# HGRN2 scores: one 128x128 product of rearranged key and query blocks per chunk in place of three small products

## The chip, the cores and the metric

The kernel runs on one core of one Trainium2 chip. The metric is the device time of one execution in microseconds (us). A core has a matrix engine, TensorE (PE in the profile; PEld is its weight load), and four others: VectorE (DVE), ScalarE (ACT), GpSimd (POOL) and SyncE (SP, which starts most transfers). Each works off its own list of instructions in order; they meet at semaphores. A matrix product takes its stationary operand as weights, streams the columns of the moving operand past it, and writes to PSUM, a small memory of eight banks; DVE and ACT copy results from there to SBUF, the working memory.

## What is computed

The reference is one inference step of a two-layer encoder trunk over 1024 prompt frames and 32 sample frames, model width 1024. Layer 0 mixes with HGRN2, a gated linear recurrence with 8 heads of 128x128 state; layer 1 with a short convolution; each is followed by an MLP. The part that the change touches is the recurrence:

```python
b = jnp.cumsum(gj, axis=-2)
qt = qj * jnp.exp(b)
kt = kj * jnp.exp(-b)
A = jnp.where(mask, jnp.einsum('bhtk,bhsk->bhts', qt, kt), 0.0)
o = jnp.einsum('bhtk,bhkv->bhtv', qt, S) + jnp.einsum('bhts,bhsv->bhtv', A, vj)
S = jnp.exp(bL[..., 0, :])[..., None] * S + jnp.einsum('bhsk,bhsv->bhkv', kj * jnp.exp(bL - b), vj)
```

The reference steps through blocks of 16 frames. The kernel takes chunks of 128 frames; the sums are the same, with other groupings of the decay factors.

## The kernel before, in words

All activations lie transposed, features on the 128 partitions, frames along the row. Layer 0 works on pairs of heads (`pr` = 0 to 3). Each pair runs four projections on TensorE (forget gate, value, query, output gate). The forget gate, query and output gate go head by head over three groups of 384, 384 and 288 columns, 24 products in a group: 8 input blocks by three passes over weights and inputs that are split in a high and a low part. Between those groups TensorE does the recurrence of the pair's two heads in six numbered steps (`step`, line 458): step 0 is `scores` of the first four chunks, step 1 `scores` of the other four and `states` of the first, step 2 the sample's scores, `outs` and `states`, step 3 `outs` and the sample's `outs`, steps 4 and 5 turn the outputs back (`o_turn`). The list `todo` (line 570) says after which group of columns a step is put: in pairs 0 to 2 step 0 of the first head follows the second column group of the second head's query projection. I name the places by letters. A is (h0,0), B is (h0,1), C is (h0,2), D is (h0,3), E is (h0,4) with (h1,0), F is (h0,5) with (h1,1), G is (h1,2). So `scores` is called at A, B, E and F: 4 calls in a pair, 16 in all, 4 chunks in a call, 64 chunks.

Within a chunk of 128 frames the scores are a 128x128 matrix (keys down, queries across), of which the lower triangle in time is wanted. One product of K and F (line 385) gives the whole matrix, and is right in the four 32x32 blocks on the diagonal. The blocks off the diagonal need other decay factors, so `carry` (lines 332 to 339) makes rescaled copies `kl` and `ql` of some key and query blocks, 128 columns for a chunk, and three small products overwrite parts of the same PSUM area (lines 388 to 390): two with 32 columns of weights and 32 moving columns, one with 64 and 64. Then one `copy_predicated` on DVE (line 391) takes what the mask allows into `at`, TensorE transposes R (`kps`, line 395), and ACT copies that to `kT` (line 397). These products are in full fp32, and each shows as two instructions in the trace.

PSUM in this stage: three banks for projections (`pj`) and a ring of five for the recurrence (`rc`, line 63). Each `rct()` takes the next of the five, and the first write to it waits until the readers of what lay there five calls earlier are done. In the program's order the calls are: A aps, kps; B aps, kps, ups; C aps, ops, ups; D ops, ups, ops; E oT, aps, kps; F oT, oT, aps, kps, ups; G as C.

The order of instructions on each engine is fixed when the program is built (the framework's scheduler may move one ahead of another where the data allow it). After layer 0 come its MLP, the convolution layer and the second MLP, which the change doesn't touch.

Of the kernel before, what the change touches and what calls it, by code (L numbers as in the profile page):

```python
# [14 lines left out]
ALU = mybir.AluOpType  # L15

P = 128
# [18 lines left out]
def trunk_kernel(  # L36
# [17 lines left out]
    nc = tc.nc  # L54
# [11 lines left out]
    def ft(name):  # L66
        return fp.tile([P, NTOK], F32, tag="ft", name=name)
# [4 lines left out]
    def rct(name="rc"):  # L72
        return rc.tile([P, 512], F32, tag="rc", name=name)
# [50 lines left out]
    def gsl(g):  # L124
        c0, n = GROUPS[g]
        return slice(c0, c0 + n), n
# [80 lines left out]
    nc.gpsimd.memset(scanm, 0)  # L207
    nc.gpsimd.memset(scanm.rearrange("p (b t) -> p b t", t=16)[:, :, 0:1], 1)
    maskf = ft("maskf")[:, : 4 * P].rearrange("p (c s) -> p c s", s=P)
    nc.gpsimd.memset(maskf, 1.0)  # L210
    nc.gpsimd.affine_select(out=maskf, in_=maskf, compare_op=ALU.is_ge, fill=0.0, base=0,
                            pattern=[[0, 4], [1, P]], channel_multiplier=-1)
    mask = hp.tile([P, 4, P], U8, name="mask", bufs=1)
# [9 lines left out]
    at = [hp.tile([P, 4, P], F32, name=f"at{i}", bufs=1) for i in range(2)]  # L223
# [100 lines left out]
    def carry(H):  # L324
        S = H.S
        H.C = ft("C")
        sf = lambda a: S[:, :, a : a + 4].unsqueeze(3).broadcast_to([P, 8, 4, 32])
        v5 = lambda t: t[:, :NPR].rearrange("p (c j t) -> p c j t", j=4, t=32)
        nc.vector.tensor_tensor(v5(H.C), v5(H.F), sf(0), op=ALU.mult)
        nc.vector.tensor_tensor(v5(H.R), v5(H.K), sf(4), op=ALU.mult)  # L330

        H.kl = fp.tile([P, 8, 4, 32], F32, tag="ft", name="kl")
        H.ql = fp.tile([P, 8, 4, 32], F32, tag="ft", name="ql")
        f2 = lambda a: S[:, :, a : a + 2].unsqueeze(3).broadcast_to([P, 8, 2, 32])
        K, F = v5(H.K), v5(H.F)
        nc.vector.tensor_tensor(H.kl[:, :, 0:2], K[:, :, 0:3:2], f2(9), op=ALU.mult)
        nc.vector.tensor_tensor(H.kl[:, :, 2:4], K[:, :, 0:2], f2(11), op=ALU.mult)
        nc.vector.tensor_tensor(H.ql[:, :, 0:2], F[:, :, 1:4:2], f2(13), op=ALU.mult)
        nc.vector.tensor_tensor(H.ql[:, :, 2:4], F[:, :, 2:4], f2(15), op=ALU.mult)
        sl = slice(NPR, NTOK)  # L340
        nc.vector.tensor_scalar(H.C[:, sl], H.F[:, sl], H.ab[:, 64:65], None, op0=ALU.mult)
        nc.vector.tensor_scalar(H.R[:, sl], H.K[:, sl], H.ab[:, 65:66], None, op0=ALU.mult)
# [34 lines left out]

    def scores(H, half):

        aps = rct("aps")  # L380
        for ci in range(4):
            c = 4 * half + ci
            o = aps[:, ci * P : (ci + 1) * P]
            sl = slice(c * P, (c + 1) * P)
            nc.tensor.matmul(o, H.K[:, sl], H.F[:, sl], start=True, stop=True)  # L385
            kl = H.kl[:, c].rearrange("p u t -> p (u t)")
            ql = H.ql[:, c].rearrange("p u t -> p (u t)")
            nc.tensor.matmul(o[0:32, 32:64], kl[:, 0:32], ql[:, 0:32], start=True, stop=True)  # L388
            nc.tensor.matmul(o[64:96, 96:128], kl[:, 32:64], ql[:, 32:64], start=True, stop=True)
            nc.tensor.matmul(o[0:64, 64:128], kl[:, 64:128], ql[:, 64:128], start=True, stop=True)  # L390
        nc.vector.copy_predicated(at[half], mask, aps.rearrange("p (c s) -> p c s", s=P))
        kps = rct("kps")
        for ci in range(4):
            c0 = (4 * half + ci) * P
            nc.tensor.transpose(kps[:, ci * P : (ci + 1) * P], H.R[:, c0 : c0 + P], ident)
        H.kT[half] = hp.tile([P, 4, P], F32, name="kT")
        nc.scalar.copy(H.kT[half], kps.rearrange("p (c s) -> p c s", s=P))
# [60 lines left out]
    def step(H, i):  # L458
        if i == 0:
            scores(H, 0)  # L460
        elif i == 1:
            scores(H, 1)
            states(H, 0)
        elif i == 2:
            s_scores(H)
            outs(H, 0)
            states(H, 1)
        elif i == 3:
            outs(H, 1)
            s_outs(H)  # L470
        elif i == 4:
            o_turn(H, H.O[:, :4], P, 4, 0)
        elif i == 5:
            o_turn(H, H.O[:, 4:], P, 4, 512)
            o_turn(H, H.Os, NSA, 1, NPR)
# [35 lines left out]
    for pr in range(HEADS // 2):  # L511
        hs = []
        for j in range(2):
            H = Head()
# [4 lines left out]
        if pr == 0:  # L519
# [3 lines left out]
            for k in range(KT):  # L523
# [7 lines left out]
                for j in range(2):  # L531
                    cs = slice(j * P, (j + 1) * P)
                    for g in range(3):
                        sl, n = gsl(g)
# [39 lines left out]
        for j in range(2):  # L574
            for g in range(3):
                q_evict(hs[j], g, proj(wt, j, g))
                if j == 1:
                    todo.pop(0)()
            carry(hs[j])
# [346 lines left out]
    with tc.tile_pool(name="cv", bufs=1) as cv:  # L926
# [3 lines left out]
        for m2 in range(4):  # L930
            wts = [wload(wg_cu_conv, 2 * m2 + j) for j in range(2)]
            cts = []
            for j in range(2):
# [13 lines left out]
                for g in range(3):  # L947
                    sl, n = gsl(g)
# [10 lines left out]
                for g in range(3):  # L959
                    sl, n = gsl(g)  # L960
# [20 lines left out]
            for j in range(2):  # L981
# [4 lines left out]
                for g in range(3):  # L986
                    sl, n = gsl(g)
# [140 lines left out]
```

## Time and profile before

| | |
|---|---|
| median of 3 runs (lowest, highest) | 2444.46 us (2442.34, 2446.22) |
| profiled execution: its time, its span | 2445.29 us, 2443.6 us |
| PE busy, share of the span | 2412.2 us, 99% |
| DVE / ACT / POOL busy | 1635.0 / 775.8 / 744.1 us |
| TensorE clock granted, mean | 0.995 of full |

The profiled execution's time is 1.69 us more than its span, which lies around the first and last instruction, and 0.83 us above the median. TensorE's instructions are pipelined, so that the durations of neighbours overlap: what one costs is read from the starts of its successors, or from the chain of waits, where each piece counts only until the next begins. Idle time of an engine that isn't the bottleneck costs nothing.

### The profile page before, as it was taken

The numbers are of one execution on the slowest core, as the hardware profiler recorded it, in microseconds if no ns is written. First come the engines' busy times: TensorE is split into PE (matmuls) and PEld (weight loads), VectorE is DVE, ScalarE is ACT, GpSimd is POOL, SyncE is SP. The second block draws the span as 40 slices with busy tenths as digits, with TensorE's granted clock in tenths as the row PEclk, the third lists the DMA queues.
The fourth block names the chain that finished last, engine by engine and source line by source line (L and its number), as shares of the span: only waits on it lengthen the run. The fifth ranks groups of instructions, "written<-read, shape, count | busy, mean of one in ns | idle before, by whom it ended". The sixth has DMA issues, their size and how long they took to land.

```text
span 2443.6 us, 39446 instructions
## 1 busy us (share of the span) xinstructions
PE 2412.2 (99%) x16548; PEld 2373.4 (97%) x16548; DVE 1635.0 (67%) x2384; ACT 775.8 (32%) x1275; POOL 744.1 (30%) x792
## 2 busy tenths in 40 slices
PE   8999999999999999999999999999999999999998
PEld 8999999989999999999999999999999999999997
DVE  8776666652887787877868533343877877868765
ACT  5121212122433334333335111023334333333334
POOL 3110100102244453444545000002253444534423
PEclk9999999999999999999999999999999999999999
DMA  4101010121011111111111111111111111111111
GB/s 151 39 21 56 22 56 22 56 91 52 28 60 44 45 51 44 61 44 44 53 44 54 42 52 44 43 53 36 41 47 44 61 44 44 53 44 61 44 35 71
DMA packets 35760, 121.99 MB, mean 50 GB/s; under 512 B 4336, under 2 KB 7552, under 8 KB 35584
## 3 DMA queue, kind: packets, MB, share of 16 engines
q1 hardware_dynamic: 33632, 113.58, 14.4%
q0 software_dynamic: 1952, 5.92, 0.7%
q8 instruction: 129, 2.11, 0.4%
q14 instruction: 47, 0.39, 0.1%
HBM read 114.09 MB, written 5.39 MB: 49 GB/s over the span
## 4 chain that ended last, share of the span: by engine, by line
PE 97%; DVE 2%; ACT 0%; issue 0%; DMA 0%; DVEq 0%; SPq 0%; ACTq 0%
PE pb L812 25%; PE pb L108 17%; PE pb L109 17%; PE pb L110 17%; PE pj L108 4%; PE pj L109 4%; PE pj L110 3%; PE v L492 1%; PE v L493 1%; PE v L494 1%; PE aps L385 1%; PE aps L390 1%; PE ops L427 1%; PE ups L402 1%; PE ops L426 1%; PE aps L388 0%
## 5 line engine op out<-in xcount | busy, mean ns | idle before, releaser
L108 PE MATMUL pb<-xh,wlo 128*128 128x384 f32 (+1 forms) x2544 | 829.3, 326 | 3.4 <-DVE hT L838 3.4
L109 PE MATMUL pb<-xl,whi 128*128 128x384 f32 (+1 forms) x2544 | 822.4, 323 | 0.0
L110 PE MATMUL pb<-xh,whi 128*128 128x384 f32 (+1 forms) x2544 | 822.4, 323 | 0.0
L709 POOL TENSOR_TENSOR hT<-hT,st 128x528 f32<-128x528 f32 x232 | 373.2, 1635 | 404.0 <-ACT st L708 404.0
L108 PEld LDWEIGHTS pb<-xh,wlo 128*128 128x128 f32 x2544 | 478.6, 188 | 8.2 <-issue 2.5
L110 PEld LDWEIGHTS pb<-xh,whi 128*128 128x128 f32 x2544 | 478.7, 188 | 0.4
L109 PEld LDWEIGHTS pb<-xl,whi 128*128 128x128 f32 x2544 | 478.7, 188 | 0.2
L821 DVE TENSOR_TENSOR hT<-hT,pb 128x528 f32<-128x528 f32 x580 | 383.4, 697 | 9.1 <-PE pb L812 0.8
L720 POOL TENSOR_TENSOR raw<-raw 128x256 f32<-128x256 f32 x232 | 209.7, 904 | 336.5 <-DVE wlo L718 322.8
L94 ACT CAST whi<-raw 128x1024 fp32r<-128x1024 f32 (+1 forms) x143 | 149.0, 1044 | 454.9 <-PE pb L110 268.0
L95 DVE TENSOR_TENSOR wlo<-raw,whi 128x1024 fp32r<-128x1024 f32 (+1 forms) x143 | 202.6, 1420 | 67.4 <-ACT whi L94 66.9
L812 PE MATMUL pb<-B,whi 128*128 128x264 f32 x1392 | 226.8, 285 | 0.0
L812 PEld LDWEIGHTS pb<-B,whi 128*128 128x128 f32 x1392 | 193.2, 189 | 0.0
L108 PE MATMUL pj<-xh,wlo 128*128 128x384 f32 (+1 forms) x536 | 177.7, 332 | 7.1 <-ACT xh L183 7.1
L109 PE MATMUL pj<-xl,whi 128*128 128x384 f32 (+1 forms) x536 | 173.4, 323 | 0.0
L110 PE MATMUL pj<-xh,whi 128*128 128x384 f32 (+1 forms) x536 | 173.1, 323 | 0.0
L787 DVE SCALAR_TENSOR_TENSOR u<-pb,nr 128x768 f32<-128x768 f32 x120 | 82.2, 704 | 124.0 <-PE pb L110 124.0
L708 ACT COPY st<-pb 128x528 f32<-128x528 f32 x232 | 133.0, 600 | 80.6 <-PE pb L812 68.9
L812 PE MATMUL pb<-T,whi 128*128 128x264 f32 x928 | 150.9, 284 | 0.0
L812 PE MATMUL pb<-Q,whi 128*128 128x264 f32 x928 | 150.7, 284 | 0.0
L812 PE MATMUL pb<-B,wlo 128*128 128x264 f32 x696 | 144.6, 289 | 3.3 <-DVE hT L821 3.3
L788 ACT ACTIVATE u<-u 128x768 f32<-128x768 f32 (+1 forms) x128 | 81.7, 642 | 161.3 <-DVE u L787 156.4
(243 smaller groups left out, 3620.3 us busy)
## 6 DMA issues: line engine op xcount, KB each, us to landing
raw<-in_wg_up_dram SPq DMA_DIRECT2D x64, 512.0 KB, 3.5
raw<-in_wg_down_dram SPq DMA_DIRECT2D x64, 512.0 KB, 3.5
raw<-in_wg_in_hgrn_dram SPq DMA_DIRECT2D x31, 512.0 KB, 4.3
raw<-in_wg_cu_conv_dram SPq DMA_DIRECT2D x16, 512.0 KB, 3.5
xk<-in_x_t_dram SPq DMA_DIRECT2D x8, 528.0 KB, 8.6
hT<-in_x_t_dram POOLq DMA_DIRECT2D x8, 528.0 KB, 7.3
raw<-in_wg_out_hgrn_dram SPq DMA_DIRECT2D x8, 512.0 KB, 4.1
raw<-in_wg_b_conv_dram SPq DMA_DIRECT2D x8, 512.0 KB, 3.6
```

The lines of the kernel that those rows point to most:

```text
L94: nc.scalar.copy(hi, raw)
L95: nc.vector.tensor_tensor(lo, raw, hi.bitcast(F32), op=ALU.subtract)
L108: nc.tensor.matmul(ps, wlo, ah, start=start, stop=False)
L109: nc.tensor.matmul(ps, whi, al, start=False, stop=False)
L110: nc.tensor.matmul(ps, whi, ah, start=False, stop=stop)
L708: nc.scalar.copy(q2(st), v)
L709: nc.gpsimd.tensor_tensor(d, d, st, op=op)
L720: nc.gpsimd.tensor_tensor(raw[:, d], raw[:, d], raw[:, o], op=ALU.add)
L787: nc.vector.scalar_tensor_tensor(d, ps, 0.0, rr, op0=ALU.max, op1=ALU.mult)
L788: nc.scalar.activation(u[:, sl], u[:, sl], AF.Square)
L812: nc.tensor.matmul(t[:, q, :QT], wf, xf[:, q * QT : (q + 1) * QT], start=start and n == 0, stop=n == 2, skip_group_check=True)
L821: nc.vector.tensor_tensor(q2(d), q2(d), v, op=op)
```

## The change

`carry` writes the same four products of blocks and factors into `kl` and `ql`, in other places: the 64-column part first, the two 32-column parts behind it. `scores` takes one more bank from the ring (`lps`) and makes one 128x128 product of the whole of `kl` and `ql` per chunk in it. Of that product three parts are used: they are copied to their places in `at` by one ACT copy (64 partitions, 4 chunks of 64 columns) and two DVE copies (32 partitions, 4 chunks of 32 columns) per call. The mask is now 1 in the lower triangle of the diagonal 32x32 blocks alone, which takes four more small memsets on POOL at the start.

```diff
-    nc.gpsimd.memset(maskf, 1.0)
+
+    nc.gpsimd.memset(maskf, 0.0)
+    for b in range(4):
+        bs = slice(32 * b, 32 * b + 32)
+        nc.gpsimd.memset(maskf[bs, :, bs], 1.0)
...
-        nc.vector.tensor_tensor(H.kl[:, :, 0:2], K[:, :, 0:3:2], f2(9), op=ALU.mult)
-        nc.vector.tensor_tensor(H.kl[:, :, 2:4], K[:, :, 0:2], f2(11), op=ALU.mult)
-        nc.vector.tensor_tensor(H.ql[:, :, 0:2], F[:, :, 1:4:2], f2(13), op=ALU.mult)
-        nc.vector.tensor_tensor(H.ql[:, :, 2:4], F[:, :, 2:4], f2(15), op=ALU.mult)
+        nc.vector.tensor_tensor(H.kl[:, :, 0:2], K[:, :, 0:2], f2(11), op=ALU.mult)
+        nc.vector.tensor_tensor(H.kl[:, :, 2:4], K[:, :, 0:3:2], f2(9), op=ALU.mult)
+        nc.vector.tensor_tensor(H.ql[:, :, 0:2], F[:, :, 2:4], f2(15), op=ALU.mult)
+        nc.vector.tensor_tensor(H.ql[:, :, 2:4], F[:, :, 1:4:2], f2(13), op=ALU.mult)
...
-        aps = rct("aps")
+
+        aps, lps = rct("aps"), rct("lps")
         for ci in range(4):
             c = 4 * half + ci
-            o = aps[:, ci * P : (ci + 1) * P]
+            cs = slice(ci * P, (ci + 1) * P)
             sl = slice(c * P, (c + 1) * P)
-            nc.tensor.matmul(o, H.K[:, sl], H.F[:, sl], start=True, stop=True)
-            kl = H.kl[:, c].rearrange("p u t -> p (u t)")
-            ql = H.ql[:, c].rearrange("p u t -> p (u t)")
-            nc.tensor.matmul(o[0:32, 32:64], kl[:, 0:32], ql[:, 0:32], start=True, stop=True)
-            nc.tensor.matmul(o[64:96, 96:128], kl[:, 32:64], ql[:, 32:64], start=True, stop=True)
-            nc.tensor.matmul(o[0:64, 64:128], kl[:, 64:128], ql[:, 64:128], start=True, stop=True)
-        nc.vector.copy_predicated(at[half], mask, aps.rearrange("p (c s) -> p c s", s=P))
+            nc.tensor.matmul(aps[:, cs], H.K[:, sl], H.F[:, sl], start=True, stop=True)
+            nc.tensor.matmul(lps[:, cs], H.kl[:, c].rearrange("p u t -> p (u t)"),
+                             H.ql[:, c].rearrange("p u t -> p (u t)"), start=True, stop=True)
+        a, l = at[half], lps.rearrange("p (c s) -> p c s", s=P)
+        nc.vector.copy_predicated(a, mask, aps.rearrange("p (c s) -> p c s", s=P))
+        nc.scalar.copy(a[0:64, :, 64:128], l[0:64, :, 0:64])
+        nc.vector.tensor_copy(a[0:32, :, 32:64], l[64:96, :, 64:96])
+        nc.vector.tensor_copy(a[64:96, :, 96:128], l[96:128, :, 96:128])
```

How the instructions stand is shown at three places. Line numbers of the changed kernel are larger by 4 to 6 (L385 is now L390, L391 now L394, L397 now L403). A product of two trace instructions is one row here.

First TensorE at place A of the first pair, where the projection before it ends and the four chunks begin; first the kernel before, one chunk and the start of the next:

```order
L110 MATMUL pj<-xh_80,whi 128x384
L385 MATMUL aps<-F,K 128x128
L388 MATMUL aps<-ql,kl 32x32 [waits DVE_49]
L389 MATMUL aps<-ql,kl 32x32
L390 MATMUL aps<-ql,kl 64x64 [waits DVE_49]
```

and now the same place in the changed kernel, to the transposes that follow (of the four chunks one stands, since they read alike):

```order
L110 MATMUL pj<-xh_80,whi 128x384
L390 MATMUL aps<-F,K 128x128
L391 MATMUL lps<-ql,kl 128x128 [waits DVE_49]
L401 MATMUL kps<-ident,R 128x128 x4
L108 MATMUL pj<-xh_73,wlo 128x288
```

Each of the four chunks has two rows of one shape in place of four rows of three shapes; nothing else on TensorE moves, here or elsewhere.

Second, ACT and DVE at the same place of the changed kernel. ACT first (the two casts are of the next projection's weights):

```order
L514 COPY vsm<-v 64x128
L94 CAST whi<-raw 128x1024 [waits DMAHW1_49,Activation_49]
L403 COPY kT<-kps 128x512 [waits PE_49]
L395 COPY at_153<-lps 64x4x64 [waits DVE_49]
L94 CAST whi<-raw 128x1024 [waits DMAHW2_49,PE_49,Activation_49]
```

DVE:

```order
L394 COPY_PREDICATED at_153<-mask,aps 128x512 [waits PE_49]
L396 COPY at_153<-lps 32x4x32 [waits PE_49,Activation_49]
L397 COPY at_153<-lps 32x4x32
L95 TENSOR_TENSOR wlo<-raw,whi 128x1024 [waits DMAHW2_49,Activation_49]
L326 TENSOR_TENSOR F<-pj,F 128x288 [waits PE_49]
```

ACT's new copy stands behind the copy of `kT` and waits for DVE's predicated copy; DVE's two new copies wait for that ACT copy. At B the scheduler has put `carry`'s first operation (now L333) between DVE's predicated copy and the new copies.

Third, TensorE at place E of the first pair, where the added bank changes who waits for whom (oT is the turned output; a wait for DVE here is one for a reader of the bank's former content):

```order
L376 MATMUL oT<-ident,O 128x128 [waits DVE_49,Activation_49]
L376 MATMUL oT<-ident,O 128x128 [waits Activation_49] x3
L390 MATMUL aps<-F,K 128x128
L391 MATMUL lps<-ql,kl 128x128 [waits DVE_49]
L401 MATMUL kps<-ident,R 128x128 [waits DVE_49,Activation_49]
```

Before, the product at that place waited for nothing and only the first transpose into `kps` waited for DVE; now the first product into `lps` does.

## Rows read from the trace of the kernel before

**Rows 1.** The page: busy time by engine, and shares of the chain that ended last.

```profile
PE 2412.2 (99%) x16548; PEld 2373.4 (97%) x16548; DVE 1635.0 (67%) x2384; ACT 775.8 (32%) x1275; POOL 744.1 (30%) x792
...
PE 97%; DVE 2%; ACT 0%; issue 0%; DMA 0%; DVEq 0%; SPq 0%; ACTq 0%
```

**Rows 2.** Busy time, steps A to F of pair 0: length, PE, PEld, DVE, ACT, POOL; clock, DMA.

```profile
80.00:128.00 48.00, 48.00 (x364) 43.16 (x363) 28.94 (x87) 9.25 (x29) 2.17 (x5) 1.00 0.16 49
```

**Rows 3.** What PE waited for, longest first: us in total, times, longest.

```profile
PE pj L108 <- ACT xh L183: 7.1, 1, 7.1
PE oT L372 <- DVE ory L365: 4.3, 1, 4.3
```

**Rows 4.** Timeline of PE at A of pair 0: start, us, engine, line, operation.

```profile
83.08 0.38 PE L385 MATMUL aps<-F,K 128*128 128x128 f32 x2
83.40 0.22 PE L388 MATMUL aps<-ql,kl 128*32 128x32 f32 x1
83.40 0.22 PE L389 MATMUL aps<-ql,kl 128*32 128x32 f32 x1
...
83.58 0.33 PE L390 MATMUL aps<-ql,kl 128*64 128x64 f32 x2
83.84 0.49 PE L385 MATMUL aps<-F,K 128*128 128x128 f32 x2
...
86.43 0.66 PE L395 MATMUL kps<-ident,R 128*128 128x128 f32 x4
```

**Rows 5.** Chain of waits at A of pair 0: start, us, what.

```profile
83.47 0.15 PE aps L388
...
83.91 0.42 PE aps L385 x2
```

**Rows 6.** Instructions on the tile aps: count, durations (least, median, most ns), first and last.

```profile
L385 PE MATMUL aps<-F,K x128: 270/275/378, 83.1 to 498.3; 128*128 128x128 f32 x128
...
L388 PE MATMUL aps<-ql,kl x128: 196/206/217, 83.4 to 498.6; 128*32 128x32 f32 x128
...
L391 DVE COPY_PREDICATED at<-mask,aps x16: 730/737/745, 86.5 to 499.1; 128x512 f32<-128x512 uint8 x16
...
L441 DVE COPY_PREDICATED ats<-masks,aps x8: 174/175/176, 99.7 to 505.3; 64x32 f32<-64x32 uint8 x8
L443 ACT COPY kTs<-aps x8: 241/243/260, 100.3 to 505.9; 64x128 f32<-64x128 f32 x8
```

**Rows 7.** Chain of waits, the 95 longest pieces: four 128x128 products in a row.

```profile
94.11 0.89 PE ups L402 x8
```

**Rows 8.** Two lines' instructions: PSUM copies on DVE and ACT.

```profile
L410 DVE COPY sn<-ups x8: 278/291/292, 95.3 to 500.6; 128x128 f32<-128x128 f32 x8
...
L397 ACT COPY kT<-kps x16: 586/587/588, 87.1 to 499.7; 128x512 f32<-128x512 f32 x16
```

**Rows 9.** Timelines of DVE, PE and ACT at E of pair 0.

```profile
111.96 0.69 DVE L366 TENSOR_TENSOR O<-ops,ory 128x512 f32<-128x512 f32 x1
...
121.15 0.56 DVE L350 TENSOR_TENSOR Y<-pj,rbc 128x384 f32<-128x384 f32 x1 [4.05 <-PE pj L110]
...
112.90 0.39 PE L385 MATMUL aps<-F,K 128*128 128x128 f32 x2
...
116.25 0.66 PE L395 MATMUL kps<-ident,R 128*128 128x128 f32 x4
...
116.94 0.59 ACT L397 COPY kT<-kps 128x512 f32<-128x512 f32 x1 [3.34 <-PE kps L395]
```

**Rows 10.** Timelines of PE and DVE at F of pair 0.

```profile
121.66 0.49 PE L385 MATMUL aps<-F,K 128*128 128x128 f32 x2
...
125.60 1.06 PE L402 MATMUL ups<-V,kT 128*128 128x128 f32 x8
...
121.63 0.74 DVE L375 SCALAR_TENSOR_TENSOR Y<-oT,hgn,Y 128x512 f32<-128x512 f32 x1
```

**Rows 11.** Timeline of DVE at the start, where the mask is made.

```profile
17.72 0.43 DVE L214 CAST mask<-maskf 128x512 uint8<-128x512 f32 x1 [0.99 <-POOL maskf L211]
```

## The prediction, made before the changed kernel ran

> **What bounds the kernel.** I read the page first. PE is busy 99% of the span, and the chain that ended last lies on PE for 97% of it [rows 1]; so time goes or comes only where TensorE's own work or its waits change. The change lies in the recurrence of layer 0, so next I took that stretch alone: from A to F of pair 0 PE is busy 48.00 of 48.00 us at a granted clock of 1.00 (the upper of its two levels, 2.4 GHz), while DVE is busy 28.94 us and ACT 9.25 us [rows 2]. The list of PE's waits has nothing at the scores: its two longest are 7.1 us for the first input block and 4.3 us for the last `o_turn`, once each [rows 3]. What is to be seen: here a microsecond off TensorE is a microsecond off the kernel, and DVE and ACT have room.
>
> Next, what the scores cost on TensorE. The timeline of one call [rows 4] is read by starts: the first K-by-F product starts at 83.08, the second chunk's at 83.84, and the transposes that follow the four chunks at 86.43. A call takes 86.43 - 83.08 = 3.35 us. The chain of waits shows where a chunk's time goes [rows 5]: the two instructions of the K-by-F product that comes behind a small product take 0.42 us, and the first small product holds the chain for another 0.15 us. Four products of one shape in a row take 0.89 us, or 0.22 each [rows 7]. So a 128-column product behind one of another shape costs about twice what it costs among its like.
>
> **What goes, and what comes on TensorE.** The trace has 128 instructions of each product line, two per product, so 64 chunks, and 16 predicated copies, so 16 calls [rows 6]. After the change a call is eight 128x128 products of one shape. None of before alternates just so between two banks; I bound a product from the nearest rows: below 0.22 us, as in the row of like products [rows 7], above 0.42 us, as for the same instruction behind a small product [rows 5]. Eight at 0.42 are 3.36 us and would gain nothing. I take 0.2225 (0.89 / 4), since weights and moving columns have the size of that row and no product of another shape comes between. A call then takes 8 x 0.2225 = 1.78 us; it saves 3.35 - 1.78 = 1.57 us, and 16 calls save 25.1 us. A delay ahead of the first product of a call, as at F behind the 32-frame transpose, stays as it is, and so do the transposes behind it.
>
> A rule of the Trainium skill speaks against this sum. What the row shows: the two 32-column products start together at 83.40 [rows 4], so they do run side by side. The skill's page TensorEngine Tiling (Array Packing), in Theoretical Speedup and Key Properties, says that small products on separate tiles of the array run in parallel, up to twice as fast where a dimension is at most 64 and four times at 32; by it three small products beat one full one, and the sum would be a small loss (the second rival). The same list in Key Properties says that changing the tiling mode drains the array. The trace agrees with both, and the second outweighs the first: the pair shares its time, and the 0.42 us behind it costs more than sharing saves.
>
> **What comes on ACT and DVE.** A call adds one ACT copy of 256 elements per partition. It lies between the rows of 128 (0.243 us [rows 6]) and 512 elements (0.587 us [rows 8]); by size about 0.36 us, 16 x 0.36 = 5.8 us in all. It adds two DVE copies of 128 elements per partition on 32 partitions: between 0.174 us (32 elements [rows 6]) and 0.291 us (128 elements on all partitions [rows 8]); I take 0.29, since it has the same number of elements per partition, so 32 x 0.29 = 9.3 us. The predicated copy and `carry`'s four products keep their sizes.
>
> These copies stand in a chain: DVE's copies wait for ACT's, which stands behind the copy of `kT`, which waits for the transposes. From the start of the transposes (116.25) to the start of the `kT` copy are 0.69 us, it takes 0.59 [rows 9], then 0.36 on ACT and 2 x 0.29 on DVE: 0.69 + 0.59 + 0.36 + 0.58 = 2.22 us until `lps` is free and `at` complete. I cost it at nothing. What covers it: at E, DVE's next work is at 121.15, for the projection behind the call, and DVE sat idle for 4.05 us before it [rows 9]; the call ends 1.57 us sooner and so does that projection, so the distance stays. At B, the copy that `carry` begins with fills DVE's wait, and at F only the `sn` copies come later, which TensorE wants a projection group later, at G. Without that cover the price is 2.22 us a call (the third rival). `at` is read two steps on.
>
> **The ring of PSUM banks.** One more bank per call shifts every later wait. I counted five calls back. F now asks six times: its `ups` takes the bank of its own first oT. DVE's read of that oT ends at 121.63 + 0.74 = 122.37, and `ups`, which started at 125.60, would start at 125.60 - 1.57 = 124.03 [rows 10]: 1.66 us of cover. At E the first product into `lps` takes the bank of D's outputs, which DVE releases at 111.96 + 0.69 = 112.65; the first product of the call starts at 112.90, the one into `lps` 0.22 later at 113.12 [rows 9]: 0.47 us of cover, the tightest place, in each of pairs 0 to 2. Between D and E no call to `scores` lies, so their distance keeps. Everywhere else a projection group lies between. If both covers were lost, `lps` would wait some tenths of a microsecond at each E.
>
> **The start and the end.** Four more memsets delay the mask on POOL; the DVE cast that waits for it started at 17.72 and had held DVE for 0.99 us [rows 11]; it is now behind one more product of the input norm, and the first call is at 83.08. Nothing. After F of pair 3 no instruction changes; the wait of 4.3 us for the last turn [rows 3] is late by the same chain as before. MLP and convolution start sooner and are as long.
>
> **The sum.** 2445.29 - 25.1 = 2420.2 us, against the profiled execution's own time, span and what lies around it. That execution is 0.83 us above the median; against the median it would be 2419.4.
>
> **The rivals.**
>
> First, part of the cost remains: not the change of shape costs, but every product has a fixed cost. From 83.84 to 86.43 [rows 4] are three chunks, 0.86 us each. Its 256 columns in all would take 0.445 us at the pace of [rows 7]; the rest, 0.415 us over four products, is 0.104 each. Two products less per chunk save 0.208 x 64 = 13.3 us: 2432.0 us. For it: four instructions fewer per chunk. Against it: like products in a row show no such cost [rows 7]. The same page of the skill has such a rule, in Instruction Overhead: about 60 cycles for each product; by that rule this rival would hold, and the trace doesn't bear it out for products of 128 columns.
>
> Second, the small products gain from sharing the array and the change costs a little: a pair of 32 side by side and one of 64 would take 96 columns' time, 96 / 128 x 0.2225 = 0.167 us, and the full one 0.2225: 0.056 x 64 = 3.6 us more, 2448.9 us. For it: the common start at 83.40 [rows 4]. Against it: a chunk's 0.86 us, which then would have to be 0.39.
>
> Third, slower: the chain of copies lands on TensorE. Its place is the next product into the bank of `lps`, or any product whose DVE read stands behind the waiting copies. Price 2.22 us a call, 16 x 2.22 = 35.5 us: 2445.3 - 25.1 + 35.5 = 2455.7 us. It decides where TensorE comes back to that bank within 2.22 us. For it: DVE waits on ACT, ACT on DVE. Against it: five calls of the ring, hence a projection group and more (over 3 us), lie between.
>
> Fourth, the saving as forecast, with waits of up to 0.5 us a call at the ring or behind DVE: 16 x 0.5 = 8 us, 2428.2 us at most. For it the 0.47 us at E; against it that PE had no such wait.
>
> **How the numbers follow.** Full saving 0.79, with waits 0.10, fixed cost per product 0.05, sharing 0.03, chain on TensorE 0.03. The likeliest gives 2420.2. Its own range is 2416 to 2424: 0.01 us on a product's pace is 1.3 us over 128 products, the runs differ by 2 us each way, and the rest is for single short waits. With most of the fourth rival the range is 2416 to 2427. A measurement of this kernel tells about 0.2% (4.9 us) from no change: faster by more are the first, second and third of these five cases, 0.94; within it the sharing, 0.03; slower 0.03.
>
> **What would show it.** Right: 16 calls of 1.78 us from first product to transposes, products of 0.22 us apiece in the chain of waits, no wait of PE at `lps`, `kps` or `ups`, DVE some 9 us busier, the time after layer 0 as before. Wrong: starts 0.33 us or more apart within a call (fixed cost), PE waiting for DVE or ACT at `lps` or at the step behind a call (ring or chain), or a wait at `at` in `outs`.

## The result, and the profile after

| | before | changed |
|---|---|---|
| median, us (lowest, highest, runs) | 2444.46 (2442.34, 2446.61, 5) | 2421.13 (2419.60, 2421.81, 5) |
| profiled execution: time, span | 2445.29, 2443.6 | 2421.13, 2419.1 |
| ratio to before, 95% interval | | 0.9902 (0.9887 to 0.9916) |

The change makes the kernel 23.3 us faster; the forecast was 2420.2 us, 2416 to 2427. The page of the changed kernel shows where the time went: PE is busy 25.8 us less than in [rows 1], DVE 9.4 us more (the forecast: some 9), ACT 3.8 us more (the forecast: 5.8; the new copies alone come to 16 x 0.365 = 5.8 us by the rows below, some of which overlap their neighbours on ACT in the record).

```profile
PE 2386.4 (99%) x16292; PEld 2362.2 (98%) x16292; DVE 1644.4 (68%) x2416; ACT 779.6 (32%) x1291; POOL 742.6 (31%) x796
```

PE's timeline at the same place A as in [rows 4], start, duration, engine, line, operation:

```profile
83.40 0.38 PE L390 MATMUL aps<-F,K 128*128 128x128 f32 x2
83.62 0.39 PE L391 MATMUL lps<-ql,kl 128*128 128x128 f32 x2
83.84 0.39 PE L390 MATMUL aps<-F,K 128*128 128x128 f32 x2
...
85.19 0.60 PE L401 MATMUL kps<-ident,R 128*128 128x128 f32 x4
85.54 0.38 PE L108 MATMUL pj<-xh,wlo 128*128 128x288 f32 x1
```

Starts are 0.22 us apart from the first product to the last, and the call takes 85.19 - 83.40 = 1.79 us in place of 3.35. The chain of waits says the same at that place; the piece of 0.42 us that stood in [rows 5] is gone:

```profile
83.78 0.22 PE lps L391 x2
84.01 0.22 PE aps L390 x2
```

The transposes behind the call are a little shorter too: from their start to the next product are 85.54 - 85.19 = 0.35 us. Before, the same product started at 86.84, 0.41 us behind the 86.43 of [rows 4]:

```profile
86.84 0.38 PE L108 MATMUL pj<-xh,wlo 128*128 128x288 f32 x1
```

So a call with its transposes gives 1.56 + 0.06 = 1.62 us, 16 of them 25.9 us. PE's longest waits, by what was waited for, have the two of [rows 3] at 7.4 and 4.3 us, and none of the list is at the scores or at what follows them:

```profile
PE pj L108 <- ACT xh L183: 7.4, 1, 7.4
PE pb L108 <- DVE hT L844: 4.6, 2, 2.4
PE oT L376 <- DVE ory L369: 4.3, 1, 4.3
```

The second row, far behind layer 0, is 1.2 us longer than before:

```profile
PE pb L108 <- DVE hT L838: 3.4, 2, 2.3
```

It is 4.6 us as well in the run below that has only the order of the old products changed, so it doesn't come from the change.

What the copies cost on their engines, from the instructions on the tile lps (count, least, median and most ns, first and last start):

```profile
L391 PE MATMUL lps<-ql,kl x128: 274/275/322, 83.6 to 473.5; 128*128 128x128 f32 x128
L395 ACT COPY at<-lps x16: 364/365/368, 86.3 to 474.7; 64x256 f32<-64x256 f32 x16
L396 DVE COPY at<-lps x16: 284/285/286, 86.7 to 475.1; 32x128 f32<-32x128 f32 x16
L397 DVE COPY at<-lps x16: 295/295/296, 87.0 to 475.4; 32x128 f32<-32x128 f32 x16
...
  DVE at L396: 6.4, 9
```

The forecast had 0.36 and 0.29 us. The last line is DVE waiting for ACT's copy, 6.4 us in 9 places: the chain through ACT and DVE is real, and it stays off TensorE. The timelines of PE and DVE at E, where the forecast saw 0.47 us of cover [rows 9]:

```profile
110.22 0.39 PE L391 MATMUL lps<-ql,kl 128*128 128x128 f32 x2
...
111.78 0.60 PE L401 MATMUL kps<-ident,R 128*128 128x128 f32 x4
```

```profile
109.06 0.69 DVE L370 TENSOR_TENSOR O<-ops,ory 128x512 f32<-128x512 f32 x1
...
113.60 0.29 DVE L397 COPY at<-lps 32x128 f32<-32x128 f32 x1
116.65 0.56 DVE L354 TENSOR_TENSOR Y<-pj,rbc 128x384 f32<-128x384 f32 x1 [2.75 <-PE pj L110]
```

DVE's read of D's outputs ends at 109.75, the product starts at 110.22: 0.47 us again. The chain ends at 113.89, 2.11 us behind the start of the transposes (2.22 forecast), and DVE is idle for 2.75 us more.

A part of the gain is given back outside the change. In the chain of waits the first product behind layer 0 starts at 499.21 in place of 524.65, 25.4 us sooner, although the first wait was 0.3 us longer; the sum of the first MLP's norm comes at 605.36 in place of 629.98, only 24.6 us sooner. Before:

```profile
524.65 0.62 PE pb L108
...
629.98 1.13 PE pb L656 x4
```

and in the changed kernel:

```profile
499.21 0.62 PE pb L108
...
605.36 1.13 PE pb L662 x4
```

Busy time by stretch (length; PE, PEld, DVE, ACT, POOL; granted clock, DMA share, GB/s) tells why. Behind the last wait of layer 0 the granted clock is 0.50, the lower of its two levels (1.2 GHz); before, for 2.8 us:

```profile
524.50:527.30 2.80, 2.80 (x10) 2.74 (x11) 2.80 (x4) 1.10 (x2) 0.00 (x0) 0.50 1.03 421
```

and in the changed kernel's profiled execution for 4.6 us:

```profile
499.10:503.70 4.60, 4.60 (x16) 4.56 (x16) 4.60 (x6) 1.07 (x1) 0.00 (x0) 0.50 0.80 317
```

1.8 us more at half the clock is 0.9 us of work that comes later. The stretch at the low clock isn't longer in the changed kernel; it lies elsewhere. The same view around it, before and in the changed kernel:

```profile
520.60:527.40 6.80, 4.12 (x15) 3.72 (x16) 6.80 (x13) 5.00 (x6) 0.00 (x0) 0.50 1.00 404
497.00:503.80 6.80, 5.96 (x20) 5.55 (x21) 6.80 (x10) 3.16 (x4) 0.00 (x0) 0.50 0.86 345
```

PE's wait began at 518.58 before and at 493.14 in the changed kernel and took 4.35 us in both. The clock fell 2.0 us into it before and 3.9 us into it here, so more of that stretch met work. That the change moved it isn't shown: in the profile of the one-shape order below the clock fell 2.2 us into the same wait. The profile of the kernel before has one more stretch at 0.50 near its end, with PE busy for 3.29 us of it (some 1.6 us of work lost), and the changed kernel's profile has none there:

```profile
2346.70:2350.10 3.40, 3.29 (x15) 3.29 (x16) 2.78 (x6) 0.00 (x0) 0.61 (x1) 0.50 0.48 159
```

### The profile page after: what moved, and what is told of

The parts are those of the page before. It is cut to its first block, busy times and chain, and to the rows that moved or that the text cites. A ratio compares the mean times of both kernels' runs of the same rounds, so it can differ in the third digit from the quotient of the medians.

```text
span 2419.1 us, 39002 instructions
## 1 busy us (share of the span) xinstructions
PE 2386.4 (99%) x16292; PEld 2362.2 (98%) x16292; DVE 1644.4 (68%) x2416; ACT 779.6 (32%) x1291; POOL 742.6 (31%) x796
## 4 chain that ended last, share of the span: by engine, by line
PE 97%; DVE 2%; ACT 0%; issue 0%; DMA 0%; DVEq 0%; SPq 0%; ACTq 0%
PE pb L818 25%; PE pb L108 18%; PE pb L110 17%; PE pb L109 17%; PE pj L108 4%; PE pj L109 4%; PE pj L110 4%; PE v L498 1%; PE v L499 1%; PE v L500 1%; PE aps L390 1%; PE lps L391 1%; PE ups L408 1%; PE ops L433 1%; PE ops L432 1%; PE oT L376 0%
```

## The experiments

Three theories of what the three small products cost were set against each other. S: a product behind one of another shape pays, as the prediction has it. B: it is the overwriting of a bank that the large product has just written. F: each product has a fixed cost, so that fewer products gain. Eight kernels ran, each beside the kernel before on the same chip; where a median of before stands below, it is of those runs.

**The small products in a bank of their own.** The changed kernel with three small products again:

```diff
-            nc.tensor.matmul(lps[:, cs], H.kl[:, c].rearrange("p u t -> p (u t)"),
-                             H.ql[:, c].rearrange("p u t -> p (u t)"), start=True, stop=True)
+            o = lps[:, cs]
...
+            nc.tensor.matmul(o[0:32, 32:64], kl[:, 64:96], ql[:, 64:96], start=True, stop=True)
+            nc.tensor.matmul(o[64:96, 96:128], kl[:, 96:128], ql[:, 96:128], start=True, stop=True)
+            nc.tensor.matmul(o[0:64, 64:128], kl[:, 0:64], ql[:, 0:64], start=True, stop=True)
...
```

(The three copies out of lps read the blocks where these products put them.)

> The changed kernel with the three small products back (32, 32 and 64 columns), but written into the bank of their own (lps) and copied from there as in the changed kernel. Theory S (a product behind one of another shape pays): a call from first product to transposes takes 3.35 us again, the time is 2445 to 2447 us. Theory B (what cost was overwriting parts of the bank that the large product had just written): the call falls to about 1.8 us, 2421 us. Theory F (a fixed cost of 0.104 us per product): 4 products per chunk as before, 2445 us; so this run sets B apart from S and F.

Measured: 2445.46 us, ratio to before 1.0005 (0.9996 to 1.0014). PE's timeline at A:

```profile
82.98 0.38 PE L390 MATMUL aps<-F,K 128*128 128x128 f32 x2
...
83.74 0.49 PE L390 MATMUL aps<-F,K 128*128 128x128 f32 x2
...
86.32 0.66 PE L405 MATMUL kps<-ident,R 128*128 128x128 f32 x4
```

A call takes 3.34 us. Another bank changes nothing: B falls. It also shows that the bank, the copies and the new mask of the changed kernel neither gain nor cost anything that can be measured; all of its gain is in the products.

**The same products in another order.** The kernel before, in each call first the large ones, then those of 32, then those of 64 columns:

```diff
+        for ci in range(4):
+            o, sl, kl, ql = ch(ci)
+            mm(o, H.K[:, sl], H.F[:, sl])
+        for ci in range(4):
+            o, sl, kl, ql = ch(ci)
+            mm(o[0:32, 32:64], kl[:, 0:32], ql[:, 0:32])
+            mm(o[64:96, 96:128], kl[:, 32:64], ql[:, 32:64])
+        for ci in range(4):
+            o, sl, kl, ql = ch(ci)
+            mm(o[0:64, 64:128], kl[:, 64:128], ql[:, 64:128])
```

(`mm` is the matmul with its flags, `ch` gives a chunk's slices; the old loop goes.)

> The kernel before, same products, same bank, no copies, but in another order within a call: first the four large products, then the eight of 32 columns, then the four of 64. Theory S: three changes of shape per call in place of twelve; four large ones 0.99 us with the change behind them, four pairs about 0.5, four of 64 about 0.6, so a call of 2.1 us and 3.35 - 2.1 = 1.25 us saved 16 times: 2424 to 2427 us. Theory F: as many products as before, no gain, 2444 us. Theory B: as many overwrites as before, 2444 us.

Measured: 2423.01 us, ratio 0.9911 (0.9897 to 0.9926). PE's timeline of the call at A (all products are made on one line now, so that those of a shape are merged; rows with 32 and 64 columns stand together as x24):

```profile
82.24 1.05 PE L384 MATMUL aps<-F,K 128*128 128x128 f32 x8
83.22 1.05 PE L384 MATMUL aps<-ql,kl 128*32 128x32 f32 x24
84.21 0.66 PE L399 MATMUL kps<-ident,R 128*128 128x128 f32 x4
```

The call takes 84.21 - 82.24 = 1.97 us, with as many products, the same bank and no copy. 16 x (3.35 - 1.97) = 22.1 us of gain by order alone: F falls, and the gain is had by doing only what S says. The expected 2.1 us was a little high, and the time came out 1 us under the range given for it.

Grouping also takes the short streams of 32 and 64 moving columns away from in front of the large products, so one more theory has to be set aside: that what cost was a weight load too long to hide behind a short stream, whatever the shape. A row of the kernel before settles it, 18 instructions (16 with 128x128 weights, the last two with 32 weight columns) that move one column each, and the next product:

```profile
34.27 1.99 PE L154 MATMUL pj<-ones,acc 128*128 128x1 f32 x18
36.20 0.39 PE L493 MATMUL v<-wlo,xh 128*128 128x256 f32 x1
```

They are (36.20 - 34.27) / 18 = 0.11 us apart, as far as the instructions of a 128-column product among its like (0.89 / 8): a short stream by itself costs the next one nothing more. What the change of shape does shows in the weight loads (PEld). Here is the load of the product at 83.84 of [rows 4] before, behind another shape, and then that of the product at 83.84 of the changed kernel, behind its like:

```profile
83.84 0.30 PEld L385 LDWEIGHTS aps<-F,K 128*128 128x128 f32 x2
```

```profile
83.73 0.30 PEld L390 LDWEIGHTS aps<-F,K 128*128 128x128 f32 x2
```

Behind its like the load starts 0.11 us ahead of its product, while the one before still runs; behind another shape the two start together, and nothing of the load is hidden. A change of shape is paid on both sides. By [rows 4] the first large product of the call, behind a projection of its own shape and ahead of a small product, takes 83.40 - 83.08 = 0.32 us to the next start; the second, between two of another shape, takes 0.42 [rows 5]; among its like it is 0.22. So each change beside a large product costs some 0.10 us.

**All small products of one shape.** The grouped order, the 64-column product split in two:

```diff
-            mm(o[0:64, 64:128], kl[:, 64:128], ql[:, 64:128])
+            mm(o[32:64, 64:128], kl[:, 96:128], ql[:, 64:128])
+            mm(o[0:32, 64:128], kl[:, 64:96], ql[:, 64:128])
```

> As the grouped order, and the 64-column product split in two with 32 weight columns and 64 moving columns each, so that all small products have one shape (128 by 32): 20 products per call in place of 16, two changes of shape. Theory S: if products on different column groups share their time, a chunk's small ones take the 96 moving columns of the busiest group, 0.167 us, and a call 0.99 + 4 x 0.167 + 0.15 = 1.8 us: 2420 to 2423 us; if they do not share it, 192 columns or 0.334 us a chunk, a call of 2.5 us, 2431 us. Theory F: one product more per chunk, 64 x 0.104 = 6.7 us slower than before, 2451 us.

Measured: 2419.88 us (2419.18 to 2421.01), ratio 0.9900 (0.9884 to 0.9917). PE's timeline at A:

```profile
81.81 1.05 PE L384 MATMUL aps<-F,K 128*128 128x128 f32 x8
82.79 0.89 PE L384 MATMUL aps<-ql,kl 128*32 128x32 f32 x32
83.61 0.66 PE L398 MATMUL kps<-ident,R 128*128 128x128 f32 x4
```

A call takes 1.80 us with 20 products. The 16 small ones, with the change of shape behind them, take 0.82 us, or 0.205 a chunk for 192 moving columns, less than the 0.2225 of 128 columns in a full product. A short weight load alone doesn't explain that: the four instructions of line 656 in the rows above stream twice 384 and twice 288 columns in 1.13 us, 0.84 ns a column, so 192 columns in two instructions would take 0.32 us one after the other. They do share their time. That is the rule of the Trainium skill's page TensorEngine Tiling (Array Packing), Theoretical Speedup, which spoke against the change; the trace agrees with it here, where the shape no longer alternates. This version needs neither the bank nor the copies nor another mask, and is level with the changed kernel: the two can't be told apart.

**Without the copies.** The changed kernel with the three copies from lps removed; the blocks of the scores below the diagonal blocks are left out.

```diff
-        nc.scalar.copy(a[0:64, :, 64:128], l[0:64, :, 0:64])
-        nc.vector.tensor_copy(a[0:32, :, 32:64], l[64:96, :, 64:96])
-        nc.vector.tensor_copy(a[64:96, :, 96:128], l[96:128, :, 96:128])
```

> The changed kernel without the three copies out of lps (the blocks below the diagonal blocks of the scores are left out and stay zero; the products are made). If the copies and their chain through ACT and DVE are hidden, as the prediction costs them: 2420 to 2422 us, same as the changed kernel. If they hold TensorE up by some tenths of a us per call: 0.3 x 16 = 5 us less, 2416 us.

Measured: 2420.90 us, 0.2 us under the changed kernel and within its runs. The copies are hidden.

**A longer chain of copies.** ACT's copy made six times in each call, then 17 times:

```diff
-        nc.scalar.copy(a[0:64, :, 64:128], l[0:64, :, 0:64])
+        for _ in range(6):
+            nc.scalar.copy(a[0:64, :, 64:128], l[0:64, :, 0:64])
```

> The changed kernel with its ACT copy made six times in each call in place of once: the chain through ACT and DVE is 5 x 0.365 = 1.8 us longer, 4.0 us from the transposes' start to the free bank. If the cover is as counted (the bank is wanted again 5.8 us after the transposes' start at B, 5.7 at F; the sn copies are wanted at C and G with over a microsecond left): no change, 2420 to 2422 us. If the cover of 2.22 us was nearly used up: 16 x 1.8 = 29 us more at most, 2450 us.

> The same with 17 ACT copies: 16 x 0.365 = 5.8 us longer, a chain of 8.0 us, more than any cover that was counted. TensorE should now wait at ups of B and lps of F for DVE or ACT (about 2 us each) and at outs of C and G for sn behind the waiting DVE copies (about 3 us): about 10 us a pair, 2450 to 2465 us. If PE never comes back to what the chain holds: 2421 us.

Measured: 2420.35 us with six, 2421.73 us (2421.41 to 2421.87) with 17. The first is as expected. The second is not: 10 us a pair were expected and none came. Timelines of PE and of DVE with 17 copies, from A to C of pair 0:

```profile
84.74 0.60 PE L402 MATMUL kps<-ident,R 128*128 128x128 f32 x4
...
90.59 1.06 PE L409 MATMUL ups<-V,kT 128*128 128x128 f32 x8
```

```profile
94.56 0.34 DVE L420 SCALAR_TENSOR_TENSOR sn<-sn,smS,ups 128x128 f32<-128x128 f32 x1
...
95.51 0.28 DVE L397 COPY at<-lps 32x128 f32<-32x128 f32 x1
95.80 0.29 DVE L398 COPY at<-lps 32x128 f32<-32x128 f32 x1
96.13 0.35 DVE L420 SCALAR_TENSOR_TENSOR sn<-sn,smS,ups 128x128 f32<-128x128 f32 x1
```

A's bank is free at 96.09, 11.35 us behind the start of A's transposes, and `ups` of B, which by my count of five had to take that bank, started at 90.59 all the same, with no wait. So in this build the bank isn't the fifth back: `ups` was given another one. Nor does DVE hold back what TensorE wants: in this build DVE's copies stand behind `sn` updates (the row at 94.56 is one), where in the changed kernel they stood ahead of them. PE's list of waits has one new entry, 0.3 us in all:

```profile
PE kps L402 <- DVE Y L379: 0.3, 1, 0.3
```

At C the chain has come up to TensorE. `outs` reads A's scores, which are complete at 96.09, and starts at 96.35; the framework's scheduler, which places instructions anew in every build, has put one product of the projection ahead of it, which in the changed kernel stands behind `ups` of C:

```profile
96.09 0.42 PE L108 MATMUL pj<-xh,wlo 128*128 128x384 f32 x1
96.35 0.38 PE L434 MATMUL ops<-V,at 128*128 128x128 f32 x2
```

So this run is the longer chain in a slightly other order. Where the chain begins to cost was not reached.

**The idle time at the end of layer 0.** The changed kernel, with products that nobody reads in TensorE's last wait of the layer:

```diff
+    fill = rct("fill")
+    v = heads[-1].V
+    for i in range(16):
+        nc.tensor.matmul(fill[:, :P], v[:, 0], v[:, 1], start=True, stop=True)
     for steps in late:
         steps()
```

> The changed kernel with 16 products of 128x128 on data at hand, into a bank that nobody reads, at the end of layer 0, where PE waits 4.35 us for the last turn (16 x 0.2225 = 3.6 us, so they end before the wait does). If it is that idle time after which the granted clock is at 0.50: the clock stays at 1.00 behind it and the 4.6 us at 0.50 become 2.3, so some 2 to 3 us less than the changed kernel, 2418 to 2419 us. If the lower clock has another cause: 2421 us, and 0.50 again in the same place.

Measured: 2418.61 us (2417.69 to 2419.66), ratio 0.9890 (0.9876 to 0.9905). The products lie where they should, by PE's timeline, and the wait behind them is 0.78 us:

```profile
493.17 3.74 PE L595 MATMUL fill<-V 128*128 128x128 f32 x32
497.69 0.63 PE L376 MATMUL oT<-ident,O 128*128 128x128 f32 x4 [0.78 <-DVE ory L369]
```

and in the stretch that stood at 0.50, by the same view as above, the clock is now at 1.00 (2.4 GHz):

```profile
499.10:503.70 4.60, 4.58 (x28) 4.56 (x29) 4.60 (x6) 1.27 (x2) 0.00 (x0) 1.00 0.83 340
```

28 PE instructions instead of 16 ran in the same 4.6 us. The median is 2.5 us under the changed kernel's, as expected, but the intervals of the two ratios overlap, and not all of it need come from here: PE's waits for `hT` far behind layer 0 are 3.0 us in this profile against 4.6.

**Both together.** The one-shape order and the same filling, two edits already shown:

> The grouped order with 32-column products alone (no bank of its own, no copies; 2419.88 us) and the same 16 products at the end of layer 0. If the two are independent: 2 to 3 us less than without them, 2417 to 2418 us; otherwise 2420.

Measured: 2418.12 us (2417.29 to 2421.98), ratio 0.9891 (0.9877 to 0.9906): 1.8 us under the order without filling, at the edge of what was expected. With the filled version above it is the fastest of the study; the two can't be told apart. Its profile doesn't repeat what the filled version's shows. The clock behind the filled wait is at 0.50 again for 3.4 us; in the one-shape order without filling it was so for 3.0 us behind the same wait:

```profile
500.50:503.90 3.40, 3.40 (x14) 3.40 (x13) 3.40 (x4) 1.07 (x1) 0.00 (x0) 0.50 0.97 395
```

```profile
498.70:501.70 3.00, 3.00 (x11) 3.00 (x11) 3.00 (x5) 1.07 (x1) 0.00 (x0) 0.50 1.03 418
```

So at this place the filling gained nothing in this execution, and where the 1.8 us come from is not shown. Two waits of 0.77 and 0.81 us stand behind the filling, in this profile as in the filled version's (0.78 and 0.81); why the clock fell in one and not in the other stays open.

## Why the prediction was right

Point by point, by its own steps:

- **TensorE bounds the stretch**: right. What was taken off PE came off the kernel; PE waits nowhere new in the stretch.
- **The price of a product among its like, 0.2225 us**: right, 0.22 to 0.23 between all starts of a call. The call was forecast at 1.78 us and took 1.79. The choice between the bounds of 0.22 and 0.42 decided the forecast, and the reason given for it holds by two runs: with the three shapes back in a bank of their own the call takes 3.34 us, with the old products in another order 1.97. One reading was too coarse: the 0.42 us is not the price behind another shape, but that between two of another shape; behind its like and ahead of another the same product takes 0.32.
- **The transposes** "stay as they are": off by 0.06 us a call, 1.0 us in all, in the change's favour.
- **The copies, at nothing**: right in size (0.365, 0.285 and 0.295 us), in the length of the chain (2.11 us against 2.22) and in the cover; without them the time is the same.
- **The ring of banks**: right in effect, by a rule that doesn't always hold. The 0.47 us at E came out to the digit because the same DVE read and the same product are there, and no wait came. But that each call takes the bank of five calls back, as the description of the kernel has it too, does not hold in the build with 17 copies; whether it does in the changed kernel isn't shown, so the covers of 1.66 us at F and elsewhere rest on a rule that can't be relied on.
- **The end of layer 0** "by the same chain as before": the wait itself is the same 4.3 us. What I didn't look at is the clock behind it, which gave back 0.9 us in the profiled execution. With it the sum is 2445.29 - 25.9 for the calls and transposes + 0.3 for the longer first wait + 0.9 = 2420.6 us, measured 2421.13. That so little is left is in part luck: further on the changed kernel's profile loses 1.2 us at the waits for `hT` and gains some 1.6 us where the kernel before has its stretch at 0.50 from 2346.70. Neither comes from the change as far as the runs show, and about 1 us stays unexplained with both, within what runs differ by.
- **The rivals**: the fixed cost (2432.0) falls by the grouped order, not by the argument from [rows 7]: an instruction with 128x128 weights takes 0.11 us with one moving column as with 128, so that a row of like products could not have shown such a cost; the sharing of the array (2448.9) is real, but too small to show while shapes alternate; the slower case (2455.7) did not come even where the bank was held for 11.35 us in place of 2.11, in an order that differs a little; of the fourth's short waits (2428.2 at most) none came.

## What to carry to other kernels

In a stretch bound by TensorE, read a product's cost from the starts of its neighbours, not from its own duration or its columns: here the same 128x128 product took 0.42 us between products of another shape and 0.22 us among its own. Before padding small products to a full one, try to put those of one shape together: order alone gave 21 of the 23 us here, with no copy and no bank (2444.32 to 2423.01 us). And look at the clock behind a wait of TensorE, not only at the wait.

## What was not expected of the hardware

Small products of 32 weight columns on different column groups share their time once they stand together: 16 of them, 768 moving columns in a call, took 0.82 us, where 512 columns in four full products take 0.89. A weight load ran 0.11 us ahead of its product behind a product of its own shape and not at all behind another. And a wait of 4.35 us on TensorE was followed by 2.8 to 4.6 us of work at a granted clock of 0.50; with the wait filled with products, none followed in one profile and 3.4 us in another. The medians with filling are 2.5 and 1.8 us lower; that this comes from the clock is shown in the first profile alone.
